# One engine instead of two for the low parts, and another order for attention's narrow products, in a two-layer encoder trunk

## The chip, the cores and the metric

The kernel runs on one core of a Trainium2 chip. The metric is the device time of one execution in microseconds (us). The engines are named as the profile names them: PE (TensorE, the matrix products), PEld (its weight loads), DVE (VectorE), ACT (ScalarE), POOL (GpSimd) and SP (SyncE, which only issues transfers here). The stationary operand of a product is loaded into PE by a load of its own; the moving operand is then streamed through it, up to 512 columns at a time.

## The reference

Two layers, each on 256 positions of 2048 channels, batch 1, all in float32:

```python
def hybrid_layer(x, ...):
    h = rmsnorm(x, norm_g)
    proj = h @ w_in
    (c_a, c_glu, c_gate, q_down, kv_down, k_pe, m_gate, g_conv, g_mla) = jnp.split(proj, idx, axis=-1)
    y_conv = conv_branch(c_a, c_glu, c_gate, ...) @ w_proj_conv   # GLU, depthwise conv of width 31, LayerNorm, SiLU, gate
    y_mla = mla_branch(q_down, kv_down, k_pe, m_gate, ...) @ w_proj_mla
    y = jax.nn.sigmoid(g_conv) * y_conv + jax.nn.sigmoid(g_mla) * y_mla
    return x + y @ w_out
```

`mla_branch` is attention with 16 heads. Queries and keys have 192 components (128 plain, 64 rotary), values 128; q comes from `q_down` (512) through `w_uq`, keys and values from `kv_down` (512) through `w_ukv`. A query sees the keys of its own chunk of 64 positions and of all chunks before it.

## The kernel before

**Products in three terms.** Each float32 matrix is split in a high part, rounded to the engine's float32r, and a low part, the rest. A product is then high times high, low times high and high times low. So each tile of weights is loaded into `raw`, ACT copies it to `hi` (`split_hi`), and the low part `lo = raw - hi` is a subtraction (`split_lo`).

**Pieces and slots.** The weights are cut into column blocks of 512 (a few of 384 and 320), and a block into *pieces* of two 128-row tiles. A piece is 12 products on PE: two halves of the positions, two tiles, three terms. `product` goes through a block piece by piece: it issues the loads, the high parts up to three pieces ahead and the low parts up to two pieces ahead (`LOAD_AHEAD, HI_AHEAD, LO_AHEAD = 4, 3, 2`), then the 12 products, then calls `background(n)`. There are five `raw` buffers, four `hi` and three `lo`. The 12 products take the moving operand from `hi` first and from `lo` last.

**The order around the products.** One call of `background` is one *slot*. Work that depends on a block (taking it out of PSUM, attention's steps, transposes) is put into a list of steps with the slot at which each is due; `late` is a list of work that is issued at the end of the slot. The convolution and the layer norm fill the rest by a budget of DVE time per slot. The class `InOrder` keeps each engine's instructions in the order in which the program issues them, so that an engine's queue is what the program wrote.

**The stages of a layer**, in order: GLU and `down` blocks; per pair of heads a `uq` and a `ukv` block with a GLU or gate block in between; then `cgate`, `mgate`, `gmla`, `pmla` (weights `wpm`), `gconv`, `pconv` (weights `wpc`, moving against `ycT`) and `wout` (weights `wo`, moving against `yT`). In `pconv` and `wout` the evacuation of PSUM is DVE's (`gate`, `xres`), and the result is turned to channels by four parking transfers (`park`: `turn_d`) and one fetching transfer (`fetch`: `turned`), issued on POOL's queue, and a 32x32 transpose on DVE. `park` of the last chunk's second half goes through SP.

**The low parts.** For most pieces DVE makes both tiles of `lo` in one instruction of 128x1024. The pieces of `wpc` and `wo` are in the set `shared`: there POOL makes tile 0 and DVE tile 1, 128x512 each.

**Attention of a pair of heads.** `attention(b)` puts its steps at fixed slots after its `ukv` block, among them `scores` at 17, `exponentials` at 19 and `values` at 32. `scores` issues, at the end of a slot, 16 products: for each of two heads three for the first 128 queries (`s0`: 256 columns, 128 columns, 256 columns) and then five of 256 columns for the others (`s1`). `maxima`, which reads both on ACT and DVE, is put into `late`. `values` issues, for each head, products of 512, 128, 256 and 256 columns into `o_ps`.

Of the kernel before, what the change touches and what calls it, by code (L numbers as in the profile page):

```python
# [11 lines left out]
F32 = mybir.dt.float32  # L12
# [7 lines left out]
P = 128  # L20
T = 2
SEQ = 256
# [83 lines left out]
def blocks_of_layer():  # L106

    s = {"win": [], "wuq": [], "wukv": [], "wpc": [], "wpm": [], "wo": []}
    for kind, i, stream in order_of_layer():
        s[stream].append(DOWN_BLOCKS[i][1] if kind == "down" else 2 * QK if kind == "uq" else 512)  # L110
    return s
# [3 lines left out]
def trunk(ctx: ExitStack, tc: tile.TileContext, xT, x, g_in, pos, win, wuq, wukv, wpc, wpm, wo, cst, rows, invf, out):  # L115
# [19 lines left out]
    pe, vec, act, gps, sp = (InOrder(e) for e in (nc.tensor, nc.vector, nc.scalar, nc.gpsimd, nc.sync))  # L135
# [20 lines left out]

    streams = {"win": (win, 16), "wuq": (wuq, 4), "wukv": (wukv, 4), "wpc": (wpc, 16), "wpm": (wpm, 16), "wo": (wo, 16)}
    taken = {}
    pieces, shared = [], set()

    def plan(layer, stream):
        ap, nk = streams[stream]
        i, at = taken.get((layer, stream), (0, 0))
        n = blocks_of_layer()[stream][i]
        mine = []
        for g in range(nk // KS):
            size = P * KS * n
            pieces.append((ap[layer, at : at + size].rearrange("(p k c) -> p k c", p=P, k=KS), n))
            at += size
            mine.append(len(pieces) - 1)  # L170
            if stream in ("wpc", "wo"):
                shared.add(len(pieces) - 1)
        taken[layer, stream] = (i + 1, at)
        return nk, n, mine

# [5 lines left out]
    loaded, highs, done, blocks_begun = {}, {}, {}, [0]  # L181
# [11 lines left out]
    def split_hi(i):  # L193
        if i >= len(pieces) or i in highs:
            return
        load(i)
        highs[i] = split_p.tile([P, KS, pieces[i][1]], F32R, tag="hi", name=f"hi{i}", bufs=4)
        singly = i < 2
        for a in range(0, KS, 1 if singly else KS):
            k = slice(a, a + 1 if singly else KS)  # L200

            for step in ("h", "w"):
                if step == "w":
                    act.copy(highs[i][:, k], loaded[i][:, k])
                    if singly:
                        split_lo(i, k)
                elif i * KS < NCT:
                    for c in range(i * KS + k.start, i * KS + k.stop):
                        first_h(c)
        for a in range(1, LOAD_AHEAD + 1):  # L210
            load(i + a)

    def split_lo(i, k=slice(0, KS)):
        if i >= len(pieces) or done.get(i, (0, 0, 0))[2] >= k.stop:
            return
        lo = done[i][1] if i in done else split_p.tile([P, KS, pieces[i][1]], F32R, tag="lo", name=f"lo{i}")
        if i in shared:
            for engine, a in ((gps, 0), (vec, 1)):
                engine.tensor_sub(lo[:, a], loaded[i][:, a], highs[i][:, a].bitcast(F32))
        else:  # L220
            vec.tensor_sub(lo[:, k], loaded[i][:, k], highs[i][:, k].bitcast(F32))
        done[i] = highs[i], lo, k.stop

    steps, clock, late, early = [], [0], [], []
    fill, budget, marks, owed, assist = deque(), {"vec": 0.0, "act": 0.0}, {}, [], []

    def at_slot(ahead, f, vec=0.0, act=0.0, first=False):  # L230
# [55 lines left out]
    def order_of_products(i, last, tardy):  # L286

        two = range(2)  # L290
        if i < 2:
            return [(t, kk, p) for kk in range(KS) for p in range(3) for t in two]
        high, low = (lambda t, p: [(t, kk, p) for kk in range(KS)]), (lambda t: [(t, kk, 2) for kk in range(KS)])
        if last:
            return high(0, 0) + high(0, 1) + high(1, 0) + low(0) + high(1, 1) + low(1)
        if tardy:
            return high(0, 0) + high(1, 0) + low(0) + low(1) + high(0, 1) + high(1, 1)
        return [e for t in two for p in two for e in high(t, p)] + low(0) + low(1)

    def product(planned, stat, evacuate, evac_at=EVAC_AT, costs=(0.0, 0.0), before=None, tardy=None):  # L300
        nk, n, mine = planned
        blocks_begun[0] += 1
        pts = [acc_p.tile([P, 512], F32, tag=f"acc{blocks_begun[0] % 2}{t}", name=f"acc{mine[0]}_{t}") for t in range(T)]

        def evac():
            for t in range(T):
                evacuate(t, pts[t][:, :n])

        for j, i in enumerate(mine):
            for a in range(HI_AHEAD + 1):  # L310
                split_hi(i + a)
                if a <= LO_AHEAD:
                    split_lo(i + a)
            hi, lo, _ = done[i]
            if before:
                before(j)
            for t, kk, part in order_of_products(i, j == len(mine) - 1, j == tardy):
                k = j * KS + kk
                sh, sl = stat(k, t)
                stationary, w = ((sh, hi), (sl, hi), (sh, lo))[part]  # L320
                pe.matmul(
                    pts[t][:, :n], stationary, w[:, kk, :],
                    start=k == 0 and part == 0, stop=k == nk - 1 and part == 2,
                )
            if j == len(mine) - 1:
                steps.insert(0, (clock[0] + 1 + evac_at, costs, evac))
            background(n)
# [206 lines left out]
    for l in range(DEPTH):  # L534
# [154 lines left out]
        def attention(b, pair_of=pair_of, ss_d=ss_d, kpe=kpe, ccq=ccq, ssq_t=ssq_t, gqk=gqk, A=A):  # L689
            p, st = pair_of(b), {}  # L690
            nope_t, rope_t, rope_k, rope_l = A.nope_t, A.rope_t, A.rope_k, A.rope_l
# [69 lines left out]
            def scores():  # L761
                s0 = s_p.tile([P, 2, 2, P], F32, tag="s0", name="s0")
                s1 = s_p.tile([P, 2, SEQ], F32, tag="s1", name="s1")

                for h in range(2):
                    qs = slice(0, P)
                    pe.matmul(s0[:, h], rope_t[:, 0, h, qs], rope_k[:, :, h, qs], start=True, stop=False)
                    pe.matmul(s0[:, h, 0, :], nope_t[:, 1, h, qs], nope_t[:, 2, h, qs], start=False, stop=False)
                    pe.matmul(s0[:, h], nope_t[:, 0, h, qs], nope_t[:, 2:4, h, qs], start=False, stop=True)
                for h in range(2):  # L770
                    qs = slice(P, SEQ)
                    terms = [
                        (rope_t[:, 0, h, qs], rope_t[:, 1, h, :]),
                        (nope_t[:, 0, h, qs], nope_t[:, 2, h, :]),
                        (nope_t[:, 0, h, qs], nope_t[:, 3, h, :]),
                        (nope_t[:, 1, h, qs], nope_t[:, 2, h, :]),
                        (rope_t[:, 0, h, qs], rope_l[:, h, :]),
                    ]
                    for n, (qa, ka) in enumerate(terms):
                        pe.matmul(s1[:, h, :], qa, ka, start=n == 0, stop=n == len(terms) - 1)  # L780
                st["s"] = s0, s1

                late.append(maxima)

            def maxima():
                s0, s1 = st["s"]
                sx = work.tile([P, 2, P], F32, tag="sx", name="sx")
                act.copy(sx, s0[:, :, 1, :])
                vec.tensor_add(sx, s0[:, :, 0, :], sx)
                for s, nkeys in ((sx, P), (s1, SEQ)):  # L790

                    vec.memset(s[:CHUNK, :, nkeys - CHUNK :], MASKED)
                nb = small.tile([P, T, 2], F32, tag="nb", name="nb")
                vec.tensor_reduce(nb[:, 0], sx, axis=AX.X, op=ALU.max, negate=True)
                vec.tensor_reduce(nb[:, 1], s1, axis=AX.X, op=ALU.max, negate=True)
                vec.tensor_mul(nb, nb, st["rs"])
                st["s"], st["nb"] = (sx, s1), nb
# [27 lines left out]
            def values():  # L825


                st["o"] = tp_p.tile([P, 2, 2, SEQ], F32, tag="tp", name="o_ps")
                pt, v = A.pt, (p["vh"], p["vl"])
                for h in range(2):  # L830
                    o = st["o"][:, h]
                    pe.matmul(o, v[0][:, 0, h, :], pt[:, :, h, :SEQ], start=True, stop=False)
                    pe.matmul(o[:, 0, P:], v[1][:, 1, h, :], pt[:, 0, h, SEQ:], start=False, stop=False)
                    pe.matmul(o[:, :, P:], v[0][:, 1, h, :], pt[:, :, h, SEQ:], start=False, stop=False)
                    pe.matmul(o[:, 0, :], v[1][:, 0, h, :], pt[:, 0, h, :SEQ], start=False, stop=True)

            def outputs():
                o = A.o_sb[:, 2 * b : 2 * b + 2, :]
# [20 lines left out]
        s1 = layer_c.tile([P, 2, SEQ], F32, tag="s1c", name="s1c")  # L859
# [491 lines left out]
```

## Time and profile before

| | |
|---|---|
| median of 3 runs | 1882.69 us (1882.26 to 1882.77) |
| span of the profiled execution | 1880.4 us, first to last instruction |
| granted TensorE clock | 1.000 of full speed, mean over the span |
| busy PE, DVE, ACT, POOL | 1872.3, 1567.8, 1366.4, 682.8 us |
| instructions | 27901, of them 8665 products |

The profiled execution's own time is given by the profile as its span alone; the 2.3 us between it and the median of the runs lie outside the first and the last instruction. All operations stand under one line of the source (a helper records them), so groups are told apart by their tiles: `lo<-raw,hi` is a low part, `acc` the PSUM of the weight products, `s` that of the scores, `o_ps` that of the values. A busy PE is no PE at its peak: products overlap, one of 512 columns is on record for about 0.39 us while the next begins earlier.

### The profile page before, as it was taken

The numbers are of one execution on the slowest core, as the hardware profiler recorded it, in microseconds if no ns is written. First come the engines' busy times: TensorE is split into PE (matmuls) and PEld (weight loads), VectorE is DVE, ScalarE is ACT, GpSimd is POOL, SyncE is SP. The second block draws the span as 40 slices with busy tenths as digits, with TensorE's granted clock in tenths as the row PEclk, the third lists the DMA queues.
The fourth block names the chain that finished last, engine by engine and source line by source line (L and its number), as shares of the span: only waits on it lengthen the run. The fifth ranks groups of instructions, "written<-read, shape, count | busy, mean of one in ns | idle before, by whom it ended". The sixth has DMA issues, their size and how long they took to land.

```text
span 1880.4 us, 27901 instructions
## 1 busy us (share of the span) xinstructions
PE 1872.3 (100%) x8665; PEld 1582.1 (84%) x8665; DVE 1567.8 (83%) x2426; ACT 1366.4 (73%) x2468; POOL 682.8 (36%) x1070
## 2 busy tenths in 40 slices
PE   9999999999999999999999999999999999999999
PEld 8988888888888888878899888888888888888887
DVE  6898988989999988766679899888899999883752
ACT  7678988888988776544557688888888878474442
POOL 1055555432200000577721555555322000006866
PEclk9999999999999999999999999999999999999999
DMA  9688878777765566668877788787777656666785
GB/s 327 219 257 265 269 241 277 258 241 245 237 199 198 190 202 223 195 227 276 284 252 216 250 270 260 258 280 244 244 240 245 193 194 203 210 203 205 237 262 168
DMA packets 140117, 445.09 MB, mean 237 GB/s; under 512 B 23808, under 2 KB 29440, under 8 KB 139968
## 3 DMA queue, kind: packets, MB, share of 16 engines
q1 hardware_dynamic: 106272, 359.89, 58.5%
q0 software_dynamic: 32832, 82.62, 13.5%
q8 instruction: 68, 1.11, 0.2%
q10 hardware_dynamic: 864, 0.80, 0.1%
q14 instruction: 81, 0.66, 0.1%
HBM read 399.18 MB, written 44.04 MB: 236 GB/s over the span
## 4 chain that ended last, share of the span: by engine, by line
PE 51%; DVE 0%; issue 0%; DVEq 0%
PE acc L126 50%; PE s L126 1%; PE o_ps L126 0%; DVE lo L126 0%; DVE xres L126 0%; DVEq L1347 0%; PE var L126 0%; PE mu L126 0%; DVEq L126 0%
## 5 line engine op out<-in xcount | busy, mean ns | idle before, releaser
L126 ACT CAST hi<-raw 128x1024 fp32r<-128x1024 f32 (+3 forms) x690 | 700.8, 1021 | 417.4 <-PE acc L126 316.2
L126 DVE TENSOR_TENSOR lo<-raw,hi 128x1024 fp32r<-128x1024 f32 (+3 forms) x690 | 791.6, 1150 | 214.3 <-PE acc L126 162.6
L126 PE MATMUL acc<-hi,hT 128*128 128x512 f32 (+2 forms) x1728 | 419.5, 382 | 0.0
L126 PEld LDWEIGHTS acc<-hi,hT 128*128 128x128 f32 x1728 | 319.7, 188 | 59.2
L126 PE MATMUL acc<-hi,h_hi 128*128 128x512 f32 (+2 forms) x864 | 260.5, 383 | 0.5 <-ACT hi L126 0.5
L126 PE MATMUL acc<-hi,h_lo 128*128 128x512 f32 (+2 forms) x864 | 260.1, 382 | 0.0
L126 ACT ACTIVATE tap<-u_t,cst 128x256 f32<-128x256 f32 x588 | 254.8, 499 | 4.3 <-DVE v_t L126 3.2
L126 POOL TENSOR_TENSOR lo<-raw,hi 128x512 fp32r<-128x512 f32 x128 | 198.6, 1562 | 124.0 <-PE acc L126 75.2
L126 POOL DMA_DIRECT2D turned<-turn_d x88 | 48.5, 552 | 513.5 <-DVE v_t L126 309.5
L126 PE MATMUL acc<-lo,h_hi 128*128 128x512 f32 (+2 forms) x864 | 229.7, 382 | 0.0
L126 PE MATMUL acc<-lo,hT 128*128 128x512 f32 (+2 forms) x864 | 229.3, 382 | 0.0
L126 DVE TENSOR_TENSOR v_t<-v_t,tap 128x512 f32<-128x512 f32 x294 | 201.8, 687 | 10.1
L126 PEld LDWEIGHTS acc<-hi,h_lo 128*128 128x128 f32 x864 | 161.0, 188 | 30.2
L126 PEld LDWEIGHTS acc<-lo,h_hi 128*128 128x128 f32 x864 | 160.5, 188 | 30.1 <-DVE lo L126 0.2
L126 PEld LDWEIGHTS acc<-lo,hT 128*128 128x128 f32 x864 | 160.6, 188 | 29.9
L126 PEld LDWEIGHTS acc<-hi,h_hi 128*128 128x128 f32 x864 | 160.0, 188 | 30.2 <-ACT hi L126 1.5
L126 DVE SCALAR_TENSOR_TENSOR v_t<-u_t,cst,v_t 128x256 f32<-128x256 f32 x372 | 159.5, 479 | 2.3
L126 POOL DMA_DIRECT2D turn_d<-gate x184 | 100.4, 553 | 149.3 <-ACT gate L126 134.0
L126 PE MATMUL acc<-hi,ycT 128*128 128x512 f32 x512 | 127.8, 389 | 0.0
L126 PE MATMUL acc<-hi,oT 128*128 128x512 f32 x512 | 127.7, 389 | 0.0
L126 PE MATMUL acc<-hi,yT 128*128 128x512 f32 x512 | 127.7, 389 | 0.0
L126 PE MATMUL acc<-hi,qkc 128*128 128x512 f32 (+1 forms) x512 | 118.7, 363 | 0.0
(170 smaller groups left out, 2320.2 us busy)
## 6 DMA issues: line engine op xcount, KB each, us to landing
raw<-in_win SPq DMA_DIRECT2D x382, 512.0 KB, 4.4
raw<-in_wpm SPq DMA_DIRECT2D x64, 512.0 KB, 3.4
raw<-in_wpc SPq DMA_DIRECT2D x64, 512.0 KB, 3.5
raw<-in_wo SPq DMA_DIRECT2D x64, 512.0 KB, 4.7
raw<-in_wukv SPq DMA_DIRECT2D x32, 512.0 KB, 3.7
turned<-turn_d POOLq DMA_DIRECT2D x56, 256.0 KB, 5.1
raw<-in_win SPq DMA_DIRECT2D x32, 384.0 KB, 4.9
raw<-in_wuq SPq DMA_DIRECT2D x32, 384.0 KB, 3.5
```

The source lines that it names most:

```text
L126: ins = getattr(self.engine, name)(*a, **k)
```

## The change

Three edits. First, the set `shared` is gone, and every low part is one subtraction on DVE:

```diff
-            if stream in ("wpc", "wo"):
-                shared.add(len(pieces) - 1)
...
-        if i in shared:
-            for engine, a in ((gps, 0), (vec, 1)):
-                engine.tensor_sub(lo[:, a], loaded[i][:, a], highs[i][:, a].bitcast(F32))
-        else:
-            vec.tensor_sub(lo[:, k], loaded[i][:, k], highs[i][:, k].bitcast(F32))
+        vec.tensor_sub(lo[:, k], loaded[i][:, k], highs[i][:, k].bitcast(F32))
```

Second, the scores are cut in two. The first head's three products for the first queries are issued where all 16 were; the other 13 wait in a new queue `woven`, which `product` empties after the first product of the next piece. In the three, the 128-column one comes last. `maxima` is issued right after the 13 products, and no longer through `late`:

```diff
                     start=k == 0 and part == 0, stop=k == nk - 1 and part == 2,
                 )
+                if woven:
+                    woven.popleft()()
...
+                def first_queries(h):
                     qs = slice(0, P)
                     pe.matmul(s0[:, h], rope_t[:, 0, h, qs], rope_k[:, :, h, qs], start=True, stop=False)
-                    pe.matmul(s0[:, h, 0, :], nope_t[:, 1, h, qs], nope_t[:, 2, h, qs], start=False, stop=False)
-                    pe.matmul(s0[:, h], nope_t[:, 0, h, qs], nope_t[:, 2:4, h, qs], start=False, stop=True)
...
+                    pe.matmul(s0[:, h], nope_t[:, 0, h, qs], nope_t[:, 2:4, h, qs], start=False, stop=False)
+                    pe.matmul(s0[:, h, 0, :], nope_t[:, 1, h, qs], nope_t[:, 2, h, qs], start=False, stop=True)
+
+                def others():
+                    for h in range(2):
...
+                            pe.matmul(s1[:, h, :], qa, ka, start=n == 0, stop=n == len(terms) - 1)
+                    first_queries(1)
+                    maxima()
+
                 st["s"] = s0, s1
-
-                late.append(maxima)
+                first_queries(0)
+                woven.append(others)
```

Third, in `values` the 128-column product of a head goes from second to last place, so that the order is 512, 256, 256, 128:

```diff
                     pe.matmul(o, v[0][:, 0, h, :], pt[:, :, h, :SEQ], start=True, stop=False)
-                    pe.matmul(o[:, 0, P:], v[1][:, 1, h, :], pt[:, 0, h, SEQ:], start=False, stop=False)
                     pe.matmul(o[:, :, P:], v[0][:, 1, h, :], pt[:, :, h, SEQ:], start=False, stop=False)
-                    pe.matmul(o[:, 0, :], v[1][:, 0, h, :], pt[:, 0, h, :SEQ], start=False, stop=True)
+                    pe.matmul(o[:, 0, :], v[1][:, 0, h, :], pt[:, 0, h, :SEQ], start=False, stop=False)
+                    pe.matmul(o[:, 0, P:], v[1][:, 1, h, :], pt[:, 0, h, SEQ:], start=False, stop=True)
```

So each 128-column product is followed by another: a weight product of 512 (384 where a `uq` block comes next), or the 512-column product of the next head. The number and size of all products stay as they were.

More of the change, by code (lines that the diff above doesn't have):

```diff
@@ L158, in trunk @@
     taken = {}
-    pieces, shared = [], set()
+    pieces = []
     def plan(layer, stream):
@@ L216, in split_lo @@
         lo = done[i][1] if i in done else split_p.tile([P, KS, pieces[i][1]], F32R, tag="lo", name=f"lo{i}")
-        if i in shared:
-            for engine, a in ((gps, 0), (vec, 1)):
-                engine.tensor_sub(lo[:, a], loaded[i][:, a], highs[i][:, a].bitcast(F32))
-        else:
-            vec.tensor_sub(lo[:, k], loaded[i][:, k], highs[i][:, k].bitcast(F32))
+        vec.tensor_sub(lo[:, k], loaded[i][:, k], highs[i][:, k].bitcast(F32))
         done[i] = highs[i], lo, k.stop
-    steps, clock, late, early = [], [0], [], []
+    steps, clock, late, early, woven = [], [0], [], [], deque()
     fill, budget, marks, owed, assist = deque(), {"vec": 0.0, "act": 0.0}, {}, [], []
@@ L763, in scores @@
                 s1 = s_p.tile([P, 2, SEQ], F32, tag="s1", name="s1")
-                for h in range(2):
+                def first_queries(h):
                     qs = slice(0, P)
                     pe.matmul(s0[:, h], rope_t[:, 0, h, qs], rope_k[:, :, h, qs], start=True, stop=False)
-                    pe.matmul(s0[:, h, 0, :], nope_t[:, 1, h, qs], nope_t[:, 2, h, qs], start=False, stop=False)
-                    pe.matmul(s0[:, h], nope_t[:, 0, h, qs], nope_t[:, 2:4, h, qs], start=False, stop=True)
[L770 to L780, printed above, removed]
+                    pe.matmul(s0[:, h], nope_t[:, 0, h, qs], nope_t[:, 2:4, h, qs], start=False, stop=False)
+                    pe.matmul(s0[:, h, 0, :], nope_t[:, 1, h, qs], nope_t[:, 2, h, qs], start=False, stop=True)
+                def others():
+                    for h in range(2):
+                        qs = slice(P, SEQ)
+                        terms = [
+                            (rope_t[:, 0, h, qs], rope_t[:, 1, h, :]),
+                            (nope_t[:, 0, h, qs], nope_t[:, 2, h, :]),
+                            (nope_t[:, 0, h, qs], nope_t[:, 3, h, :]),
+                            (nope_t[:, 1, h, qs], nope_t[:, 2, h, :]),
+                            (rope_t[:, 0, h, qs], rope_l[:, h, :]),
+                        ]
+                        for n, (qa, ka) in enumerate(terms):
+                            pe.matmul(s1[:, h, :], qa, ka, start=n == 0, stop=n == len(terms) - 1)
+                    first_queries(1)
+                    maxima()
                 st["s"] = s0, s1
-                late.append(maxima)
+                first_queries(0)
+                woven.append(others)
             def maxima():
```

## The prediction

> **What bounds the kernel now.** I read the page first, then PE's waits, then the time order of PE around each wait, then what the engines it waited for were doing.
>
> ```profile
> span 1880.4 us, 27901 instructions
> PE 1872.3 (100%) x8665; PEld 1582.1 (84%) x8665; DVE 1567.8 (83%) x2426; ACT 1366.4 (73%) x2468; POOL 682.8 (36%) x1070
> ...
> PE acc L126 <- POOL lo L126: 1.7, 3, 0.7
> PE warm L126 <- DVE zeros L126: 1.2, 1, 1.2
> PE acc L126 <- DVE lo L126: 0.9, 2, 0.5
> PE acc L126 <- ACT hi L126: 0.5, 1, 0.5
> ```
>
> PE is busy for 1872.3 of 1880.4 us. Work on another engine can only be worth what PE now waits, and that is little: five waits for a low part, three of them POOL's. PE's time order shows each (start, length; the bracket is the idle time before the row):
>
> ```profile
> 839.83 1.52 PE L126 MATMUL acc<-hi,ycT 128*128 128x512 f32 x6
> 842.04 1.20 PE L126 MATMUL acc<-lo,ycT 128*128 128x512 f32 x4 [0.70 <-POOL lo L126]
> ...
> 822.24 0.96 PE L126 MATMUL acc<-lo,ycT 128*128 128x512 f32 x3 [0.46 <-DVE lo L126]
> ...
> 886.44 0.97 PE L126 MATMUL acc<-lo,yT 128*128 128x512 f32 x3 [0.56 <-POOL lo L126]
> ...
> 908.93 0.73 PE L126 MATMUL acc<-lo,yT 128*128 128x512 f32 x2 [0.43 <-POOL lo L126]
> ...
> 1780.48 0.97 PE L126 MATMUL acc<-lo,ycT 128*128 128x512 f32 x3 [0.47 <-DVE lo L126]
> ...
> L126 PE MATMUL acc<-hi,hT 128*128 128x512 f32 x1536 | 383.6, 389 | 0.0
> ...
> 1611.55 0.23 PE mu L126 x2
> 1611.78 29.94 PE acc L126 x132
> 1641.96 136.03 PE acc L126 x600
> ```
>
> The last three rows, of the chain that ended last, give the pace without a disturbance: 136.03 / 600 = 0.2267 us for a product of 512 columns, though each is on record for 0.389. So an undisturbed successor begins 0.389 - 0.227 = 0.162 us before the printed end, and a stop costs the bracket plus 0.162. Behind a stop the first products are slower too: three take 0.97 where 0.389 + 2 x 0.227 = 0.843 is normal. In all: 822: 0.46 + 0.16 + 0.12 = 0.74; 842: 0.70 + 0.16 + 1.20 - 1.07 = 0.99; 886: 0.56 + 0.16 + 0.13 = 0.85; 909: 0.43 + 0.16 + 0.11 = 0.70; 1780: 0.47 + 0.16 + 0.13 = 0.76. **Sum 4.04 us.** All five lie in the stages of `wpc` and `wo`, where the low parts are shared.
>
> **Part one: all low parts on DVE.** Why was the low part late? (DVE and POOL in order of time.)
>
> ```profile
> 814.49 6.00 DVE L126 TENSOR_TENSOR yT<-turned,yT 128x512 fp32r<-128x512 f32 x2
> 820.41 1.77 DVE L126 TENSOR_TENSOR lo<-raw,hi 128x512 fp32r<-128x512 f32 x1
> ...
> 816.14 5.50 POOL L126 TENSOR_TENSOR lo<-raw,hi 128x512 fp32r<-128x512 f32 x4
> ...
> 839.06 1.63 POOL L126 DMA_DIRECT2D turn_d<-gate  x3 [2.04 <-issue]
> 840.71 2.53 POOL L126 TENSOR_TENSOR lo<-raw,hi 128x512 fp32r<-128x512 f32 x2
> ...
> L126 DVE TENSOR_TENSOR yT<-turned,yT x16: 677/680/5408, 814.5 to 1805.8; 128x512 fp32r<-128x512 f32 x16
> ...
> 885.09 3.78 POOL L126 TENSOR_TENSOR lo<-raw,hi 128x512 fp32r<-128x512 f32 x3
> 907.58 3.77 POOL L126 TENSOR_TENSOR lo<-raw,hi 128x512 fp32r<-128x512 f32 x3
> ```
>
> Two causes, both POOL's. At 820, a DVE subtraction that has a median of 0.68 us ends only 4.7 us late, while POOL makes four low parts one after another; DVE's own low part stands behind it. The longest of these subtractions, 5.41 us, belongs to the stop at 1780. At 842, 886 and 909, POOL's low parts stood behind transfers on its queue (here three issues, the first after 2.04 us of waiting) and then came in a row, too late.
>
> The Trainium skill, "SBUF — State Buffer", section "SBUF: two separate sides", says that DVE and POOL share a pair of ports as an exclusive lock for one whole instruction, taken also by a DVE operation with two SBUF inputs. By that the DVE subtraction would wait for one POOL subtraction; the row above shows it held through three in a row. Both readings end when POOL subtracts no more, and the sum is the same.
>
> ```profile
> L126 DVE TENSOR_TENSOR lo<-raw,hi 128x1024 fp32r<-128x1024 f32 x478 | 582.4, 1219 | 53.8 <-PE acc L126 22.1 <-issue 11.0 <-ACT hi L126 9.2
> L126 DVE TENSOR_TENSOR lo<-raw,hi 128x512 fp32r<-128x512 f32 x132 | 135.2, 1036 | 136.6 <-PE acc L126 122.9 <-issue 6.8 <-POOL lo L126 6.1
> ...
> L126 POOL TENSOR_TENSOR lo<-raw,hi 128x512 fp32r<-128x512 f32 x128 | 198.6, 1562 | 124.0 <-PE acc L126 75.2 <-ACT hi L126 33.6 <-POOL lo L126 9.8
> ...
> 560.00:650.00 90.00, 90.00 (x399) 74.53 (x398) 86.67 (x123) 72.80 (x126) 0.00 (x0) 1.00 0.58 193
> 787.00:809.10 22.10, 22.10 (x99) 18.32 (x98) 12.04 (x13) 8.77 (x9) 18.14 (x19) 1.00 0.72 237
> 854.00:876.00 22.00, 22.00 (x99) 18.22 (x98) 19.59 (x19) 11.03 (x13) 14.01 (x14) 1.00 0.80 251
> ```
>
> It removes 128 POOL subtractions, 198.6 us of an engine that is no bound. DVE's 128 halves become wholes of 1.219 us. From the disturbed mean, 1.036, that adds 128 x 0.183 = 23 us; from an undisturbed half, near 0.68 like the `yT` subtraction of the same size, 69 us. I take the second as the careful end: 8 pieces a block add 8 x 0.54 = 4.3 us to 22 us, so DVE goes from 12.0 to 16.3 there (the windows' busy columns are PE, PEld, DVE, ACT, POOL). In the fullest, 19.6 + 4.3 = 23.9 us would pass 22, but 4.7 of the 19.6 are the same hold by POOL and go. Between 560 and 650 DVE makes every low part at 86.67 of 90 us and PE loses nothing: that is the nearest row, and it says DVE alone is enough.
>
> What is queued behind the new, longer subtraction: at a block's end DVE has 1.22 plus two pairs of `gate` operations (4 x 0.69), 3.98 us in a slot of 12 x 0.227 = 2.72. The low part then comes 1.26 us late, covered by being made two pieces, 5.4 us, ahead. The queues of POOL lose what stood between their transfers; that makes chunks come back earlier, and PE waits for none of them. Bounds: -4.04 us if all five stops go, 0 if others take their place. **I take -4.0.**
>
> **Parts two and three: the narrow products.** Their number stays: per pair of heads two of 128 columns in `s`, two in `o_ps`, 16 pairs, 64. What does one cost?
>
> ```profile
> 1153.40 0.19 PEld L126 LDWEIGHTS o_ps<-pv 128*128 128x128 f32 x1
> 1153.63 0.30 PEld L126 LDWEIGHTS o_ps<-pv 128*128 128x128 f32 x2
> ...
> 1143.49 1.89 PE s L126 x16
> 1145.38 8.19 PE acc L126 x36
> 1153.56 1.16 PE o_ps L126 x8
> ```
>
> The eight of `o_ps` take 1.16 us: two of 512 at 0.227 and four of 256 at 0.115 (the `mu` row) leave 0.12 for each of 128, where half of a 256 would be 0.06. So one loses 0.06, 64 lose 3.8 us: that is all that an order could win. The load rows say why. The load at 1153.40 starts with the 512-column product; the next, at 1153.63, only when the 128-column product begins. The one behind it starts 0.30 - 0.19 = 0.11 later. One load at a time is ahead, a load takes its turn for 0.11, and a narrow product streams for half of that. The load of *its successor* is bare, whatever the successor's width, and the 512 columns ahead of it did not help here either (that row is 512, 128). No row has 128 in front of 512. Bounds: 0 to -3.8; the load rows are nearest, and by them it is **0**.
>
> What the cut adds: PE now returns from `s` to weight products twice per pair. After `s`, 36 products take 8.19 us where 36 x 0.2267 is 8.16: 0.03 us a return. After `mu` 132 take 29.94 against 29.92: 0.02. Bounds 0 and 16 x 0.03 = +0.5; **+0.3**.
>
> `maxima` moves behind the next piece's high and low parts on ACT and DVE.
>
> ```profile
> DVE sx L126 <- ACT sx L126: 26.3, 16, 2.5
> ...
> 170.00:360.00 190.00, 190.00 (x933) 163.84 (x932) 166.91 (x294) 165.22 (x366) 104.00 (x208) 1.00 0.80 262
> ```
>
> DVE waits 1.6 us a pair there now; the low part will fill 1.2 of it. The scores end about 1.89 + 0.23 us into the slot, and what is queued behind (the next low part) is needed two pieces on. `exponentials` is due two slots later. Cost on PE: 0, hidden by those 5.4 us; without them each pair would cost up to the 1.6.
>
> **Sum:** -4.0 + 0 + 0.3 = -3.7 against the profiled 1880.4, so a span of 1876.7. The median stands 2.3 above the span; 1882.69 - 3.7 = **1879.0**. A measurement of this kernel tells about 0.2%, 3.8 us, from no change: the forecast lies on that edge.
>
> **Rivals.**
> *The order pays.* If a 128-column product in front of a wide one loses nothing, another 3.8 us goes: 1875.2. For it: nothing in the trace has that pair. Against: the load rows. Half of it would be 1877.1.
> *Only POOL's queue was the cause.* If the 5.4 us on DVE at 820 and 1780 come again without POOL's subtractions, only 0.99 + 0.85 + 0.70 = 2.5 is won: 1880.5. Against: they coincide with POOL's row to within a few tenths.
> *DVE is late at the block ends (slower).* If the 3.98 us in a slot of 2.72 are not caught up, each of the 16 block ends of these stages stops PE for some 0.8 us as the present stops do: +13 - 4.0 + 0.3 makes 1892. It decides once DVE is more than 5.4 us behind. Against: one slot's surplus of 1.3 us meets 1.5 us of slack in the next.
> *POOL's transfers are held up by DVE (slower).*
>
> ```profile
> L126 POOL DMA_DIRECT2D turn_d<-qk x128 | 70.8, 559 | 21.5 <-ACT qk L126 16.8 <-issue 2.5 <-DVE s L126 2.2
> L126 POOL DMA_DIRECT2D turn_d<-gate x184 | 100.4, 553 | 149.3 <-ACT gate L126 134.0 <-DVE gate L126 8.1 <-issue 5.0
> ```
>
> If an issue had to wait for a low part of 1.22 us, the last chunk of a stage (four parking, two fetching issues) would come 7.3 us late, past the 5.4 us cover, 1.9 us at each of three stage ends: +5.7 - 3.7, 1884.7. Against: beside DVE's whole low parts in attention an issue takes 559 ns, in the shared stages 553. The same skill section tells of such a hold on descriptors, beside fast DVE copies; no row here shows it.
>
> **How the numbers follow.** Forecast 0.70 (1878.4 to 1879.4, half of it past the edge); the order pays, in part or in full, 0.12; queue only 0.11; the two slower ones 0.04 and 0.03. Faster by over 0.2%: 0.37 + 0.12 = 0.49; within: 0.33 + 0.11 = 0.44; slower 0.07. The range reaches from half of the order's gain, 1876.8, to the queue-only case with the returns at their bound, 1880.9.
>
> **What would show it.** In the trace after: no wait of PE for `lo` past the start; `yT` subtractions all near 0.68; DVE's low parts all near 1.22; no POOL `lo`; `o_ps` still near 1.16 before the next products begin, or, if the order pays, 0.2 less. I am wrong if PE waits for DVE's `lo` in `pconv` or `wout`, or if the attention stages shorten.

## The result, and the profile after

The changed kernel takes 1879.0 us (median of 17 runs, 1878.48 to 1879.59), the kernel before 1882.59 (17 runs). The ratio is 0.9982, 95% interval 0.9974 to 0.9989: 3.6 us, 0.19%, faster. The profiled execution's span went from 1880.4 to 1877.2 us.

The page of the changed kernel, first lines:

```profile
span 1877.2 us, 27404 instructions
PE 1872.3 (100%) x8665; PEld 1583.6 (84%) x8665; DVE 1578.2 (84%) x2426; ACT 1364.4 (73%) x2468; POOL 486.6 (26%) x942
```

All that PE waits for in it, over the whole span:

```profile
PE warm L126 <- DVE zeros L126: 1.2, 1, 1.2
```

The five waits for a low part are gone, and no other has come. POOL is busy 196 us less, DVE only 10 us more. Why so little is seen in DVE's groups with shapes kept apart, and in the list of `yT`'s instructions (shortest, median and longest in ns):

```profile
L126 DVE TENSOR_TENSOR lo<-raw,hi 128x1024 fp32r<-128x1024 f32 x606 | 738.3, 1220 | 182.6 <-PE acc L126 134.1 <-issue 22.5 <-ACT hi L126 11.9
...
L126 DVE TENSOR_TENSOR yT<-turned,yT x16: 677/682/687, 815.5 to 1802.4; 128x512 fp32r<-128x512 f32 x16
```

The 606 whole subtractions take 1.22 us on average, as the 478 did before, and DVE's other work is no longer held: `yT`'s longest went from 5408 to 687 ns. DVE stays far from full in these stages (columns as in the prediction):

```profile
787.40:809.10 21.70, 21.70 (x97) 17.97 (x96) 12.30 (x12) 8.38 (x9) 5.51 (x10) 1.00 0.75 241
...
852.60:874.40 21.80, 21.80 (x98) 18.02 (x97) 16.17 (x20) 10.57 (x13) 3.33 (x6) 1.00 0.77 242
```

And the chain that ended last, for one pair of heads, in order of time (start, length, what):

```profile
1175.14 0.29 PE s L126 x3
1175.44 0.29 PE acc L126
1175.73 1.49 PE s L126 x13
1177.22 8.05 PE acc L126 x35
1185.27 1.11 PE o_ps L126 x8
1186.38 23.30 PE acc L126 x108
1209.68 0.29 PE s L126 x3
```

From one block of scores to the next it is 1209.68 - 1175.14 = 34.54 us. The same two blocks in the chain of the kernel before:

```profile
1177.96 1.89 PE s L126 x16
...
1212.43 1.89 PE s L126 x16
```

There it is 34.47. The same products take longer in the new order: 0.07 us a pair, 16 pairs, 1.1 us. So the change is a gain of some 4 us and a loss of one. From the start of the first product of the scores to that of the last product of all, a stretch without the kernel's start, the kernel before takes 1702.76 us and the changed one 1699.70: 3.06 less.

### The profile page after: what moved, and what is told of

Read it like the earlier page. It is cut to its first block, busy times and chain, and to the rows that moved or that the text cites. A ratio compares the mean times of both kernels' runs of the same rounds, so it can differ in the third digit from the quotient of the medians.

```text
span 1877.2 us, 27404 instructions
## 1 busy us (share of the span) xinstructions
PE 1872.3 (100%) x8665; PEld 1583.6 (84%) x8665; DVE 1578.2 (84%) x2426; ACT 1364.4 (73%) x2468; POOL 486.6 (26%) x942
## 3 DMA queue, kind: packets, MB, share of 16 engines
q8 instruction: 68, 1.11, 0.2%
## 4 chain that ended last, share of the span: by engine, by line
PE 100%; DVE 0%; DVEq 0%; issue 0%
PE acc L126 97%; PE s L126 2%; PE o_ps L126 1%; PE warm L126 0%; PE mu L126 0%; PE var L126 0%; DVE xres L126 0%; DVEq L1348 0%; DVE zeros L126 0%
## 5 line engine op out<-in xcount | busy, mean ns | idle before, releaser
L126 DVE TENSOR_TENSOR lo<-raw,hi 128x1024 fp32r<-128x1024 f32 (+3 forms) x690 | 815.2, 1183 | 206.7 <-PE acc L126 152.7
L126 PEld LDWEIGHTS acc<-hi,yT 128*128 128x128 f32 x512 | 96.1, 188 | 20.0
```

What stands on the lines that cost most here:

```text
L126: ins = getattr(self.engine, name)(*a, **k)
```

## The experiments

Spans of single profiled runs carry a jitter of their own: at the very start PE waits between 0 and 1.2 us for the first high parts, from run to run. Where a microsecond matters I therefore compare the time of one pair of heads, which repeats to 0.01 us for pairs with the same work behind them, and the stretch from the first product of the scores to the last product. Runs given with one time were taken once.

**Each part alone.** The first edit alone (`dve_only`):

```diff
+        vec.tensor_sub(lo[:, k], loaded[i][:, k], highs[i][:, k].bitcast(F32))   # for all pieces; scores and values as before
```

> The first edit alone: all low parts on DVE, scores and values in their old order. Theory: the five stops of PE (4.0 us) go, and the new order of the narrow products costs some 0.07 us a pair of heads (the time from one block of scores to the next is 34.54 us in the changed kernel, 34.47 before), 1.1 us in all; so this kernel is faster than the changed one: span 1876.1 us, median 1877.9. Rival, the order is free: span 1877.2, median 1879.0. Rival, the order pays and DVE's load costs: span above 1878.

Measured: median 1878.06 us of 9 runs (1877.87 to 1878.75), ratio to the kernel before 0.9974 (0.9964 to 0.9984), span 1877.0. Beside the wait for `zeros`, PE waits in it only once, 1.2 us for `hi` at the start. Its chain:

```profile
1175.34 1.89 PE s L126 x16
1177.22 8.19 PE acc L126 x36
1185.41 1.16 PE o_ps L126 x8
1186.57 23.24 PE acc L126 x108
1209.81 1.89 PE s L126 x16
```

A pair takes 34.47 us. The first edit does all of the good: the stretch from the first scores on takes 1698.63 us, 4.13 less than before and 1.07 less than in the changed kernel. Its median is 0.9 us under the changed kernel's, but the two intervals against the kernel before overlap, so this rests on the traces.

The other two edits alone (`order_only`), POOL and DVE sharing as before:

```diff
+        if i in shared:
+            for engine, a in ((gps, 0), (vec, 1)): ...   # as before
```

> The second and third edit alone: POOL and DVE still share the low parts of wpc and wo. Theory: the five stops in the stages of wpc and wo stay (some 4 us) and 1.1 us comes on top: span 1881.5. Rival, the order is free: 1880.4. Rival, the order pays: below 1880.

Measured: 1883.77 us, span 1882.0. Its PE waits:

```profile
PE acc L126 <- POOL lo L126: 1.4, 2, 0.7
...
PE acc L126 <- DVE lo L126: 0.9, 2, 0.5
```

And two blocks of scores in its chain:

```profile
1179.16 0.29 PE s L126 x3
...
1213.70 0.29 PE s L126 x3
```

Four of the five stops behind low parts stay, and a pair takes 34.54 us as in the changed kernel. One time of 1883.77 says nothing, since the kernel before ranged from 1881.32 to 1884.13 beside it. The stretch from the first scores on does: 1703.47 us, 0.71 more than before, with the order's 1.07 in it and one stop fewer. The order alone wins nothing and makes the kernel a little slower.

The first and the third edit (`values_order`):

```diff
+                    pe.matmul(o[:, :, P:], ...); pe.matmul(o[:, 0, :], ...); pe.matmul(o[:, 0, P:], ..., stop=True)   # 512, 256, 256, 128
```

> The first and the third edit: only the values' narrow product goes to the end of its head's four. Theory: its eight products and the start of the next take 0.014 us a pair more than with the old order, 0.2 us in all over the first edit alone: span 1876.3. Rival, all of the cost of the new order sits here: 1877.2. Rival, the order pays here: below 1876.0.

Measured: 1878.45 us, span 1876.6. Its chain:

```profile
1184.99 1.11 PE o_ps L126 x8
1186.11 23.30 PE acc L126 x108
1209.41 1.89 PE s L126 x16
```

From the values to the next scores 1209.41 - 1184.99 = 24.42 us, with the first edit alone 1209.81 - 1185.41 = 24.40: 0.02 us a pair, about as expected. The values' own block is shorter by 0.05 (1.11 for 1.16), and the products behind it take that back (23.30 for 23.24): the bare load has only moved across the border of the block.

**What in the new scores costs.** The cut kept, but the narrow product in the middle of its three (`cut_middle`):

```diff
-                    pe.matmul(s0[:, h], nope_t[:, 0, h, qs], nope_t[:, 2:4, h, qs], start=False, stop=False)
-                    pe.matmul(s0[:, h, 0, :], nope_t[:, 1, h, qs], nope_t[:, 2, h, qs], start=False, stop=True)
+                    pe.matmul(s0[:, h, 0, :], nope_t[:, 1, h, qs], nope_t[:, 2, h, qs], start=False, stop=False)
+                    pe.matmul(s0[:, h], nope_t[:, 0, h, qs], nope_t[:, 2:4, h, qs], start=False, stop=True)
```

> The first edit and the cut of the scores, but with the 128-column products of the scores in the middle of their three, in front of 256 columns, and the values in their old order. It tells two reasons for the cost of the new scores apart. Theory a, PE pays for each return from narrow to wide products and the cut makes two of one: 0.03 us a pair over the first edit alone, span 1876.6. Theory b, the 128-column product is dearer in front of 512 columns than in front of 256: no more than with the first edit alone, span 1876.1.

Measured: 1878.0 us, span 1876.2. Timed again, as the version that may beat both (`cut_middle_timed`, the same kernel):

> The kernel with all low parts on DVE, the cut scores, and the narrow products in the middle as before, timed. Blocks of scores take 0.02 us a pair less here than with the first edit alone and 0.09 less than in the changed kernel in what this kernel left earlier (34.45, 34.47 and 34.54 us from one block to the next), 1.4 us in all against the changed one: median 1877.7. Rival, the start's jitter (up to 1 us from run to run) covers it: 1878.0 to 1878.1 as with the first edit alone.

Measured: median 1877.77 us of 9 runs (1877.17 to 1878.12), ratio to the kernel before 0.9974 (0.9964 to 0.9984), span 1876.2. The chain of the timed one:

```profile
1174.68 0.35 PE s L126 x3
1175.03 0.23 PE acc L126
1175.26 1.54 PE s L126 x13
1176.80 7.94 PE acc L126 x35
1184.74 1.16 PE o_ps L126 x8
1185.89 23.24 PE acc L126 x108
1209.14 0.35 PE s L126 x3
```

A pair takes 34.46 us, 0.08 less than in the changed kernel; 16 times that is the 1.2 us between the two medians, so this is the better version of the two. Against the first edit alone its median is 0.3 us lower, within the spread of either's runs, so only the 0.01 to 0.02 us a pair of the chains speak for it. A second return to wide products costs nothing; theory a, which is also my prediction's price for the cut, falls. The loss of the changed kernel sits behind the second group. At the first, the three products and the wide one behind them take 0.59 us together for 0.58 here: the wide one's 0.29 for 0.23 is what the three ahead of it have saved (0.29 for 0.35). At the second, the 13 and the 35 behind them take 9.54 for 9.48: 0.05 saved, and 0.11 lost.

Theory b was that a narrow product is dearer in front of a wide one. The scores uncut, one narrow product before 256 and one before 512 (`uncut_last`):

```diff
+                # ten of 256 columns first, then for either head: 256, 256, 128; then the weight products of 512
```

> The first edit, the scores uncut but in another order: the ten of 256 columns first, then 256, 256, 128 for either head, so that one narrow product stands in front of 256 and one in front of a weight product of 512. Values in their old order. Theory b (a narrow product is dearer in front of 512): 0.03 to 0.04 us a pair more than with the first edit alone, 34.50 from one block of scores to the next where that has 34.47. Rival (the dearer thing is the second return from narrow to wide): 34.47 or less.

Measured: 1878.01 us, span 1876.2. Its chain:

```profile
1174.68 1.85 PE s L126 x16
1176.53 8.21 PE acc L126 x36
...
1209.14 1.85 PE s L126 x16
```

34.46 us a pair, no more than with the first edit alone. Theory b as a rule falls too. And every narrow product between two of 256 (`best_order`):

```diff
+                    pe.matmul(o[:, :, P:], ...); pe.matmul(o[:, 0, P:], ...); pe.matmul(o[:, 0, :], ..., stop=True)   # 512, 256, 128, 256; scores as in cut_middle
```

> All low parts on DVE, the scores cut, and every 128-column product in front of one of 256 columns with a product of 512 behind that: in the scores 256, 128, 256, in the values 512, 256, 128, 256. Theory: a narrow product is cheapest there; the pair of heads takes no more than with the narrow ones in the middle of the scores alone (34.45 us from one block of scores to the next, 34.54 in the changed kernel), so 1.4 us under the changed kernel: median 1877.6. Rival, the place in the values does not matter: the same as with the cut scores alone, 34.45. Rival, no gain beyond the start's jitter: median 1878.1 as with DVE alone.

Measured: median 1878.06 us of 10 runs, ratio 0.9976 (0.9967 to 0.9986), span 1876.7. Its chain:

```profile
1175.08 0.35 PE s L126 x3
...
1209.56 0.35 PE s L126 x3
```

34.48 us, 0.02 more than with the old order of the values: not the 34.45 of the theory and the first rival, and the median is the second rival's, no gain over the first edit alone. The place of a narrow product moves a pair of heads between 34.46 and 34.54, and none of my rules says how; why the same end (256, 256, 128, then 512) is cheap in one kernel and dear in the changed one stays open.

No narrow product at all (`no_narrow`):

```diff
-                    pe.matmul(s0[:, h, 0, :], nope_t[:, 1, h, qs], nope_t[:, 2, h, qs], ...)
+                    pe.matmul(s0[:, h], nope_t[:, 1, h, qs], nope_t[:, 2:4, h, qs], ...)   # and o[:, :, P:] for o[:, 0, P:]
```

> The first edit alone, with no 128-column product left: each is widened to 256 columns, which adds the product of the two low parts (more work, a finer result). Theory, a load takes its turn for 0.11 us and a narrow product therefore costs nearly what one of 256 does (0.12): the pair's scores go from 1.89 to 1.92 us, the values from 1.16 to 1.17, with what follows 34.50 to 34.53 from one block to the next, 0.9 us in all above the first edit alone. Rival, a narrow product costs its 0.06 and a fixed loss of 0.06 more that the wide one has too: 0.06 each, 64 of them, 3.8 us.

Measured: 1879.69 us, span 1877.9. Its chain:

```profile
1175.87 1.91 PE s L126 x16
...
1185.97 1.17 PE o_ps L126 x8
1187.14 23.28 PE acc L126 x108
1210.41 1.91 PE s L126 x16
```

34.54 us a pair: four products of twice the width cost 0.07 us together, 0.02 each, and 0.04 of the 0.07 stands only in the 108 products behind the values (23.28 for 23.24), where the order alone moves as much. A narrow product already costs nearly what one of 256 columns does, as the load rows said; the rival, 0.24 a pair, is out.

**Why the low parts were late.** The kernel before, with parking transfers on SP's queue (`park_sp`):

```diff
-                return turn(src, 512, None, then=use, then_costs=costs)
-            turn(src, 512, None, then=use, then_costs=costs, fetch_at=2, at=4, queue=sp if t else gps)
+                return turn(src, 512, None, then=use, then_costs=costs, queue=sp)
+            turn(src, 512, None, then=use, then_costs=costs, fetch_at=2, at=4, queue=sp)
```

> The kernel before, with the parking transfers of pconv and wout on SP's queue and no longer on POOL's. Theory, two causes: the three stops at 842, 886 and 909, where POOL's low part stood behind transfers, go (2.5 us), and the two behind the held DVE subtraction stay unless POOL's run falls elsewhere: span near 1878. What can spoil it: the loads of weights stand behind the parking transfers on SP, which wait for DVE, and PE then waits for a high part. Rival, POOL was late for its own slowness: the three stops stay, 1880.

Measured: 1878.67 us, span 1876.6, where the theory gave 1878. All that PE waits for in it beside `zeros`, and POOL in order of time where the stop at 822 was:

```profile
PE acc L126 <- ACT hi L126: 0.6, 1, 0.6
```

```profile
814.63 1.29 POOL L126 TENSOR_TENSOR lo<-raw,hi 128x512 fp32r<-128x512 f32 x1 [1.43 <-PE acc L126]
817.35 1.47 POOL L126 TENSOR_TENSOR lo<-raw,hi 128x512 fp32r<-128x512 f32 x1 [1.43 <-PE acc L126]
820.07 1.81 POOL L126 TENSOR_TENSOR lo<-raw,hi 128x512 fp32r<-128x512 f32 x1 [1.25 <-ACT hi L126]
```

All five stops are gone with POOL still making its half, and the stretch from the first scores on takes 1698.63 us, as with the first edit alone. POOL's low parts come singly here, one a slot of 2.72 us, with 1.25 to 1.43 us of room ahead of each. Before, they came four in a row at 816, behind eight parking transfers:

```profile
811.75 4.38 POOL L126 DMA_DIRECT2D turn_d<-gate  x8 [0.84 <-DVE gate L126]
```

The kernel before has nine such rows of four in the two layers, and this run none (once three); with the rows the long holds of DVE's `yT` go too (1.79 us at most). The two causes of the prediction were one: POOL's queue.

POOL's subtractions as a mere disturbance (`pool_beside`), DVE making all low parts:

```diff
+        if i in shared:
+            for c in (slice(0, 256), slice(256, 512)):
+                gps.tensor_sub(idle, loaded[i][:, 0, c], highs[i][:, 0, c].bitcast(F32))
```

> The first edit alone, and beside it POOL still subtracts for the pieces of wpc and wo, as two instructions of 256 columns, into a tile that nobody reads. PE depends on DVE's low parts alone. Theory, two causes: POOL's run of subtractions holds DVE's subtraction of yT again for several us, so DVE's low part behind it comes late and PE stops near the ends of the two pconv stages (0.7 us each), and the three stops behind POOL's transfers do not come back: 1.5 us above the first edit alone. Rival, only the wait for POOL's own low parts mattered: yT near 0.68 us throughout, no stop.

Measured: 1905.64 us, span 1903.8, 27 above the first edit alone. Two of the rows of what PE waits for, and POOL and then DVE in order of time:

```profile
PE acc L126 <- ACT yT L126: 12.7, 2, 7.6
...
PE acc L126 <- DVE lo L126: 2.0, 4, 1.4
```

```profile
865.62 4.56 POOL L126 TENSOR_TENSOR idle<-raw,hi 128x256 f32<-128x256 f32 x4
870.12 1.23 POOL L126 DMA_DIRECT2D turned<-turn_d  x2
...
876.42 0.71 DVE L126 STREAM_TRANSPOSE turned<-turned 128x512 f32<-128x512 f32 x1 [8.49 <-DMA turned<-turn_d]
```

Neither theory: no long hold of `yT` (1.23 us at most) and no stop in `pconv`, but the fetching transfer of the last chunk is issued at 870.12, behind four subtractions, DVE waits 8.49 us for it at the head of its queue, and PE stops for `yT` at the start of `wout`, in both layers. It also stops four times for DVE's low parts, in `wout` and behind it. Around the long stops the granted clock falls as well, so that more is lost than the wait (columns as in the prediction; the clock is the third number from the end):

```profile
877.84:881.42 3.58, 3.58 (x8) 2.62 (x9) 3.58 (x5) 2.52 (x3) 1.50 (x2) 0.50 0.45 142
881.42:900.00 18.58, 18.58 (x83) 15.34 (x83) 13.12 (x11) 7.59 (x11) 16.87 (x20) 1.00 0.70 237
```

PE waits here from 870.25 to 877.84; the clock is at half from 874.59 to 881.42, so the first eight products take 3.58 us. Half clock comes three times, and PE works through 11.2 us of it: by that some 5.6 of the 27 us, an estimate. The added work is heavier than what POOL had (two instructions of 1.11 us on average a piece, 284 us, against 199). The same with the parking on SP (`pool_beside_sp`):

```diff
+                return turn(src, 512, None, then=use, then_costs=costs, queue=sp)   # and queue=sp for the last chunk
```

> All low parts on DVE, POOL's idle subtractions of 256 columns beside them into a tile that nobody reads, and the parking transfers of pconv and wout on SP's queue. POOL beside DVE alone cost 26 us, with DVE waiting 8.5 us for a fetching transfer that POOL issued behind its subtractions. Theory, POOL's queue order is what hurts: with the four parking issues a chunk's half gone from it, the fetches come earlier, and most of the 26 us go: under 1882. Rival, two engines on the same memory ports hurt by themselves: still above 1890. The fetching transfers stay on POOL, so some late ones may remain.

Measured: 1883.39 us, span 1881.6. It has one row of waits of weight:

```profile
PE acc L126 <- ACT yT L126: 2.6, 2, 1.5
```

22 of the 27 us go with the parking transfers, a little less than the theory said (under 1882), while POOL subtracts as much beside DVE as before (300 us, 284 in `pool_beside`). So the queue is what hurts, and the rival is out. Where PE still stops, at 870 and 872, DVE's transposes had waited 3.75 and 2.76 us for fetching transfers, which stayed on POOL; 3.4 us at half clock follow. That the fetches leave all of the rest is likely, and not shown by a run without them.

**How much room DVE has.** Every shared low part made twice (`dve_twice`):

```diff
+        for _ in range(2 if i in shared else 1):
+            vec.tensor_sub(lo[:, k], loaded[i][:, k], highs[i][:, k].bitcast(F32))
```

> The first edit alone, with every low part of wpc and wo made twice over on DVE (the same values): DVE's load there is 9.8 us a block more. In the changed kernel DVE is busy 9.4 to 16.2 of 21.8 us a block; so five blocks of sixteen in all come above 24 us, the rest stay below or near the time. Theory, being two pieces ahead hides any surplus that the next blocks can make good, and only what passes it stops PE: 5 to 20 us above the first edit alone, all of it in the blocks with gate operations. Rival, a low part that takes two slots' worth of time is always late: 16 blocks, over 30 us. Rival, no stop: DVE has the room.

Measured: 1899.19 us, span 1897.4, 20.4 above the first edit alone: just over the top of what the theory gave. PE's waits for low parts, and busy times in one stretch:

```profile
PE acc L126 <- DVE lo L126: 14.1, 19, 1.5
```

```profile
766.00:788.00 22.00, 20.61 (x90) 16.30 (x89) 21.66 (x26) 11.04 (x14) 0.00 (x0) 1.00 0.44 144
```

With DVE full (21.66 of 22.00) PE stops for its low parts, up to 1.5 us at a time. Two of the 19 stops, at 921 and 944, lie in `wout` outside the blocks with gate operations, where the theory had none. So the slower rival of the prediction is a real mechanism: it is there with the low parts made twice and absent with them made once; where between the two it begins was not tried.

## Why the prediction was right, point by point

The forecast of 1879.0 is the median measured, and the mechanism of the first edit held; that it came out exact is luck. With the order's measured price the same sum gives -4.0 + 1.1 = -2.9, or 1879.8, and the traces say -3.06 from the first scores on. The rest of the 3.6 us lies in the start's jitter and within what the runs leave open, 2.1 to 4.9 us.

*The five stops, -4.0:* right. The first edit alone has none of them, no wait has taken their place, and the stretch from the first scores on is 4.13 us shorter. *Their cause:* the prediction's "two causes, both POOL's" was half right. The hold of DVE was real in the trace, but followed from POOL's row of four, which followed from its queue; moving the parking transfers alone took all five away. The rival "only POOL's queue was the cause" had the right cause and the wrong price: it let the two holds return.

*DVE's load:* the careful end, 4.3 us a block, was not reached in either block shown: 12.3 where 16.3 was given, 16.2 in the fullest where it came to 19.2, and 10 us in all. The term missed how much of DVE's time before was spent held by POOL. It also had the hold in the wrong place: no long `yT` subtraction lies between 854 and 876 (all four take 0.68 us there), and what was stretched are the low parts, whose eight halves took 13.00 us where the eight whole ones take 9.52 in the changed kernel. It cost nothing, because DVE had the room either way.

*The order, 0, and the returns, +0.3 (bound +0.5):* this is the term of the sum that was mis-sized. It measured +1.1 (34.54 - 34.47 = 0.07, 16 times; 1.07 from the first scores on), over its bound. That a narrow product gains nothing from a wide one behind it held; that the order could cost, I did not allow for: the bounds of that term ended at 0. The price of a return, taken from the rows after `s` and `mu`, was not the mechanism, since the cut with the narrow products in the middle costs no more than no cut. What makes the new order dear stays open. The range's upper end has a slip of its own: the queue-only case with the returns at their bound is 1882.69 - 2.54 + 0.5 = 1880.7, not 1880.9.

*maxima:* no stop, as said. DVE's wait for ACT's copy went only from 26.3 to 17.7 us, as this row of the changed kernel's waits shows, less than the 1.2 us a pair that I gave:

```profile
DVE sx L126 <- ACT sx L126: 17.7, 16, 1.2
```

The second head's scores for the first queries, which `sx` needs, now come last of the 16, and ACT's copy waits 14.4 us in all for the scores where it waited 6.5 before. That this is why DVE's wait shrank less was not tried by itself.

*The hold of DVE:* its 5.4 us came again, twice, with the order alone, which keeps the rows of four. Beside single subtractions of 512 columns `yT` takes 1.79 us at most. So the long hold goes with the row; but a row alone is not enough. With POOL's idle subtractions of 256 columns there are rows of eight and more, and `yT` takes 1.23 us at most, 1.67 with the parking on SP's queue. There some 0.08 us lie between one subtraction and the next, while the first three at 816 follow without a gap; whether it is the gap that lets DVE in was not tried. The Trainium skill, "SBUF — State Buffer", section "SBUF: two separate sides", has the lock last for one instruction: that fits the rows of 256 columns and not the 5.4 us. The held descriptors that the same section of the Trainium skill tells of did not show: an issue of `turn_d<-gate` takes 553 ns in the changed kernel, as before, and with DVE's whole low parts in `pconv` and `wout` PE waits for no transfer.

## What to carry to other kernels

When a stop is put down to a slow helper engine, look at what stands ahead of the late instruction in that engine's queue: here 4 us hung on transfers issued there, and moving either the transfers or the work cured it. A product so narrow that the next weight load outlasts it costs nearly what one twice as wide does; reordering such products moves the loss across block borders, and a gain must be read over the block and the products behind it together. A term whose bounds end at zero on one side needs a reason for that side.

## What the runs showed of the hardware

Widening a 128-column product to 256 cost 0.02 us each, where half of a 256-column product's 0.115 us would be 0.06. A pair of heads with the same products took 34.46 to 34.54 us by the order alone, the scores and what follows them repeating to 0.01 us from pair to pair, and part of the difference lies up to ten products behind the narrow one (8.05 for 7.94 us over 35). What sets this I could not settle. A DVE subtraction of 0.68 us took 5.4 beside four POOL subtractions of 512 columns in a row. The granted clock, 1.00 in the other kernels from 7.3 us at the latest to the last product, fell to half for 3.4 to 6.8 us around waits of PE of 1.1 to 7.6 us in the two kernels with POOL's idle subtractions, and not in `dve_twice`, whose 19 waits are of 0.4 to 1.5 us.
